# S5 steps of a four-branch trunk moved from GpSimd to VectorE, TensorE and ScalarE; convolution and rotary stage read PSUM

## The chip, the core and the metric

One core of one Trainium2 chip runs the whole program. The metric is the device time of an execution in microseconds; three executions of the kernel before give a median of 1277.6 us (1272.61 to 1278.52). "TensorE", "VectorE", "ScalarE", "GpSimd" and "SyncE" are PE, DVE, ACT, POOL and SP in the profile.

## The reference

A trunk of two layers over 272 tokens (16 learned ones and 256 of the input) of width 1024. Each layer normalizes, projects once into all inputs of four branches, runs the branches, weighs each by a sigmoid gate, adds them, projects, and ends with a squared-ReLU MLP of width 4096. The branches:

- *HGRN2*: attention with a decay per key channel; forget gate `f = lb + (1 - lb) * sigmoid(f_raw)`, key `1 - f`.
- *SSD* (Mamba-2): a causal convolution of four taps over 1024 channels, silu, then attention with a scalar decay.
- *S5*: a diagonal complex state space, 32 groups of 16 channels with 64 states: `x_t = a x_(t-1) + B u_t`, `y_t = Re(C x_t) + d * u_t`, then gelu and a gated linear unit.
- *Retention*: queries and keys are rotated (`x1 cos - x2 sin`, `x1 sin + x2 cos` on halves of 32 channels), then attention with a fixed decay.

All is float32.

## The kernel before

**Projections.** Weights come in 336 chunks of 128 x 1024 (`chunk`, line 307). ScalarE rounds a chunk to its high half (`whi`, L325), VectorE subtracts that from the chunk (`wlo`, L327), and TensorE multiplies (`gemm`, lines 333 to 351): per 128 rows of input, high x high (L344), high x low (L345) and low x high (L347), 24 matmul records a chunk, into one of three PSUM banks `g`. Other matmuls use the PSUM banks `ma`, `mb` (two each) and `mc` (one), and are in plain float32, which the profile shows as two records each.

**Order.** The program is written once in order; a planner then orders each engine's queue by priority and by its own estimates of when operands are there. The split of weights has a raised priority (`PS`, line 321). Each engine runs its queue in order. Loads of weights go through SyncE's queue; small loads (S5's parameters `raw`, the rotary tables) through ScalarE's.

**S5.** Time is cut into 68 steps of four tokens; the 512 channels are four blocks b of 128. `s5_params` (line 833, layer 0 only) computes powers of the state factor by well over a hundred small VectorE operations. Per block, `s5_prep` (line 995) loads the block's B and C, and forms outer products of parameters and B or C: `bs` and `cx[0]` on VectorE, `cx[1]` on GpSimd (`outer`, L1011 to L1013, 512 wide). `s5_table` (line 978) makes the rotation table E by six products of 288 on GpSimd (L987 to L992). TensorE and ScalarE form the short convolution `ki` (L1042 to L1048) and transpose `bs` (`bi`, L1059). `s5_run` (line 1099) multiplies the input W by `bi` into PSUM, turns it by E (L1115 to L1120), scans the two parts (L1128), turns back (L1132 to L1137; L1132 and L1135 on GpSimd), and sums `ki`, `cx` and the states into PSUM `yp` (L1143, L1146); VectorE adds `du`, the input times d, made on GpSimd (L1139, L1148). After two blocks `s5_out` (line 1150) applies gelu (L1154) and moves rows of 32 partitions into channel order by 16 copies, half on VectorE (L1160), half on ScalarE (L1162). At the end of `s5` all four parts are split into halves (L362, L364). Tiles of a block have one buffer each, so blocks follow one another. S5 runs beside the projections of the gates; its result is used much later, in `glu`. Block 0 of layer 1 is prepared in layer 0 (line 462).

**HGRN2 in.** `hgrn_in` (line 1185): after tanh on ScalarE, VectorE scales and shifts the forget gate (L1201) and GpSimd makes `1 - f` (L1202).

**Convolution.** In `ssd_in` (line 1329), for each of eight chunks ScalarE copies the projection out of PSUM (L1401) and makes the last tap (L1402); VectorE adds three taps from the copy (L1405).

**Rotary.** `ret_in` (line 1479): ScalarE copies four projections out of PSUM (L1489); then the two tables are loaded (L274), and GpSimd multiplies by the sine table with halves exchanged (four products of 32 partitions, L1496), by the cosine table (L1497), and adds (L1500, L1501).

Of the kernel before, what the change touches and what calls it, by code (L numbers as in the profile page):

```python
# [233 lines left out]
class Net:  # L234
# [760 lines left out]
    def s5_prep(self, l, b, after=None):  # L995
# [39 lines left out]
        nc.scalar.activation(nb, bs[:, 1, :, 3], AF.Copy, scale=-1.0)  # L1035

        def kd(pe=nullcontext(), act=nullcontext()):

            kp = self.bank("mc")[0:32].rearrange("p (q d x) -> p q d x", q=4, d=4)
            with pe:  # L1040
                for q in range(4):
                    nc.tensor.matmul(kp[:, q], lhsT=bs[:, 0, q, 3], rhs=cx[0][:, q, 0:4], start=True, stop=False)  # L1042
                    nc.tensor.matmul(kp[:, q], lhsT=nb[:, q], rhs=cx[1][:, q, 0:4], start=False, stop=True)
            for s in range(1, 4):
                g.memset(ki[32 * s:32 * s + 32, :, 0:s], 0.0)
            with act:
# [33 lines left out]
    def s5(self, l, W):  # L1080
        yf = self.slot(6, [128, 4, 68, 4])
        for b in range(4):
# [7 lines left out]
            self.s5_run(l, b, W, prep, Y[:, 4 * (b % 2):4 * (b % 2) + 4])  # L1090
            if b % 2:
                self.s5_out(b - 1, Y, yf)
        yf = yf.rearrange("p a c s -> p a (c s)")
        gh, gl = self.slot(9, [128, 4, T], F32R), self.slot(7, [128, 4, T], F32R)
        for i in range(4):
            self.split(yf[:, i], gh[:, i], gl[:, i])
        return gh, gl

    def s5_run(self, l, b, W, prep, Y):
# [38 lines left out]
        du = a1  # L1138
# [11 lines left out]
    def s5_out(self, b, Y, yf):  # L1150

# [3 lines left out]
        G = Y.rearrange("p (a q c) -> p a q c", a=2, q=4)  # L1155
        for q in range(4):
# [28 lines left out]
    def hgrn_in(self, l, raw, r, norm, t0):  # L1185
# [6 lines left out]
        for i in range(4):  # L1192
# [6 lines left out]
            nc.scalar.activation(f, f, AF.Tanh, scale=0.5)  # L1199
            a, b = (0.5, 0.5) if l == 0 else (self.omlb[:, i:i + 1], self.lb[:, i:i + 1])  # L1200
# [277 lines left out]

    def ret_in(self, l, u, t0):
        nc = self.nc  # L1480
        g = nc.gpsimd
        qk = self.slot(1, [128, 4, T])
        if t0:
            g.memset(qk[:, 0:2, 0:t0], 0.0)
# [5 lines left out]
        rot = [self.slot(k, [128, 4, T]) for k in (8, 2)]  # L1490
        for i in range(2):
            self.load_after(rot[i], self.io["rot"].rearrange("p (c k t) -> p c k t", c=2, k=4)[:, i], qk[:, 0:1, 0:1])
        sw = self.slot(13, [128, 4, T])
        for q in range(4):
            a, b = slice(32 * q, 32 * q + 32), slice(32 * (q ^ 1), 32 * (q ^ 1) + 32)
# [2 lines left out]
        qf, k = self.slot(14, [128, 4, T]), self.kpad[1]
        q = qf[:, 0:2]
        g.tensor_tensor(out=q, in0=qk[:, 0:2], in1=sw[:, 0:2], op=ALU.add)  # L1500
        g.tensor_tensor(out=k[:, :, 0:T], in0=qk[:, 2:4], in1=sw[:, 2:4], op=ALU.add)  # L1501
# [50 lines left out]
```

## Time and profile before

| | us |
|---|---|
| median of three executions | 1277.6 |
| lowest, highest | 1272.61, 1278.52 |
| the profiled execution, as timed | 1277.68 |
| its span, first to last instruction | 1275.9 |
| TensorE busy | 1216.1 |
| VectorE busy | 893.0 |
| ScalarE busy | 694.2 |
| GpSimd busy | 411.0 |

The profile is of one execution. Busy time of an engine is the time in which at least one of its instructions runs; matmuls overlap, and their ends are modelled. "Granted clock" is the share of full speed that the chip allowed TensorE. A stretch is given in microseconds from the start of the span. The S5 blocks of layer 0 run between about 150 and 300 us, those of layer 1 between about 800 and 925 us.

### The profile page before, as it was taken

How to read it: one execution, taken by the hardware profiler on the slowest of the kernel's cores; microseconds unless marked ns; L12 is line 12 of the kernel's file. 1: busy time of each engine (PE TensorE's matmuls, PEld its weight loads, DVE VectorE, ACT ScalarE, POOL GpSimd, SP SyncE). 2: the span in 40 equal slices, each digit the busy share in tenths (PEclk: the TensorE clock that was granted, in tenths of full speed). 3: DMA queues.
4: the chain of work that ended last, by engine and by line, in shares of the span. 5: the costliest groups of instructions: out<-in, count | busy, mean ns of one | idle time of the engine just before them, and what ended most of it. 6: DMA issues, size and time to landing. Idle time of an engine off the chain costs nothing.

```text
span 1275.9 us, 24312 instructions
## 1 busy us (share of the span) xinstructions
PE 1216.1 (95%) x9534; PEld 1174.6 (92%) x9534; DVE 893.0 (70%) x1480; ACT 694.2 (54%) x1219; POOL 411.0 (32%) x422
## 2 busy tenths in 40 slices
PE   8999998879999989999989999988999998999997
PEld 7999897879999989999979998987999998999996
DVE  8999989885637675544468995898656487655444
ACT  7446746443745665544455558354647546665442
POOL 2452467668002142200024333575170031322001
PEclk9999999989999989999989999998999998999998
DMA  6423232344354535555434332333444553555552
GB/s 238 160 98 104 101 123 99 108 136 145 135 175 173 176 110 178 173 175 178 170 108 143 126 123 97 123 111 114 146 150 149 184 179 136 169 188 189 182 184 98
DMA packets 53187, 186.69 MB, mean 146 GB/s; under 512 B 6096, under 2 KB 7248, under 8 KB 53072
## 3 DMA queue, kind: packets, MB, share of 16 engines
q1 hardware_dynamic: 50480, 179.40, 41.2%
q10 hardware_dynamic: 2592, 5.74, 1.4%
q8 instruction: 75, 1.23, 0.4%
q14 instruction: 40, 0.33, 0.1%
HBM read 184.06 MB, written 1.05 MB: 145 GB/s over the span
## 4 chain that ended last, share of the span: by engine, by line
PE 76%; DVE 13%; issue 4%; POOL 3%; ACT 2%; DMA 1%; SPq 0%; DVEq 0%; ACTq 0%; POOLq 0%
PE g L347 22%; PE g L344 22%; PE g L345 22%; DVE wlo L327 3%; PE mb L726 1%; PE ma L1263 1%; PE mb L717 1%; POOL S L1496 1%; DVE h L604 1%; DMA s5a<-in_bc 1%; DVE big_npom L601 1%; DVE s5a L1012 1%; ACT whi L325 1%; PE ma L726 1%; PE mb L1109 1%
## 5 line engine op out<-in xcount | busy, mean ns | idle before, releaser
L327 DVE TENSOR_TENSOR wlo<-wst,whi 128x1024 fp32r<-128x1024 f32 x336 | 438.5, 1306 | 259.1 <-PE g L347 220.8
L325 ACT ACTIVATE whi<-wst 128x1024 fp32r<-128x1024 f32 x336 | 355.8, 1060 | 365.3 <-PE g L345 287.6
L347 PE MATMUL g<-xh_u,wlo 128*128 128x272 f32 (+1 forms) x1024 | 299.7, 294 | 16.0 <-DVE wlo L327 15.8
L344 PE MATMUL g<-xh_u,whi 128*128 128x272 f32 (+1 forms) x1024 | 299.5, 293 | 0.6 <-ACT early L1068 0.4
L345 PE MATMUL g<-xl_u,whi 128*128 128x272 f32 (+1 forms) x1024 | 297.8, 291 | 0.0
L344 PE MATMUL g<-S,whi 128*128 128x272 f32 (+1 forms) x832 | 236.0, 288 | 4.6 <-ACT S L541 4.1
L347 PE MATMUL g<-S,wlo 128*128 128x272 f32 (+1 forms) x808 | 230.0, 288 | 1.7 <-DVE wlo L327 1.7
L345 PE MATMUL g<-S,whi 128*128 128x272 f32 (+1 forms) x768 | 220.4, 289 | 2.2 <-DVE S L552 1.9
L347 PEld LDWEIGHTS g<-xh_u,wlo 128*128 128x128 f32 x1024 | 195.7, 192 | 21.0 <-DVE wlo L327 18.2
L344 PEld LDWEIGHTS g<-xh_u,whi 128*128 128x128 f32 x1024 | 196.5, 192 | 2.6 <-ACT early L1068 0.7
L345 PEld LDWEIGHTS g<-xl_u,whi 128*128 128x128 f32 x1024 | 196.5, 192 | 1.5 <-issue 1.2
L344 PEld LDWEIGHTS g<-S,whi 128*128 128x128 f32 x832 | 157.1, 190 | 5.3 <-ACT S L541 4.5
L347 PEld LDWEIGHTS g<-S,wlo 128*128 128x128 f32 x808 | 151.9, 189 | 2.6 <-DVE wlo L327 2.2
L345 PEld LDWEIGHTS g<-S,whi 128*128 128x128 f32 x768 | 145.8, 190 | 4.1 <-DVE S L552 4.0
L345 PE MATMUL g<-xl_npm,whi 128*128 128x272 f32 (+1 forms) x512 | 147.7, 291 | 1.2 <-DVE xl_npm L552 1.2
L344 PE MATMUL g<-xh_npm,whi 128*128 128x272 f32 (+1 forms) x512 | 143.6, 289 | 2.4 <-ACT xh_npm L541 2.4
L347 PE MATMUL g<-xh_npm,wlo 128*128 128x272 f32 (+1 forms) x496 | 140.5, 288 | 0.0
L345 PEld LDWEIGHTS g<-xl_npm,whi 128*128 128x128 f32 x512 | 99.1, 193 | 1.9 <-DVE xl_npm L552 1.7
L344 PEld LDWEIGHTS g<-xh_npm,whi 128*128 128x128 f32 x512 | 96.7, 193 | 2.9 <-ACT xh_npm L541 2.9
L677 POOL TENSOR_TENSOR acc<-acc,tmp 128x272 f32<-128x272 f32 (+1 forms) x48 | 38.9, 828 | 186.0 <-DVE tmp L676 186.0
L347 PEld LDWEIGHTS g<-xh_npm,wlo 128*128 128x128 f32 x496 | 94.2, 192 | 0.2
L507 POOL TENSOR_TENSOR tmp<-tmp 128x272 f32<-128x272 f32 (+1 forms) x64 | 45.7, 714 | 137.3 <-DVE wlo L327 79.5
(377 smaller groups left out, 2184.4 us busy)
## 6 DMA issues: line engine op xcount, KB each, us to landing
wst<-in_w SPq DMA_DIRECT2D x336, 512.0 KB, 3.5
S<-in_rot ACTq DMA_DIRECT2D x4, 544.0 KB, 6.8
s5a<-in_bc ACTq DMA_DIRECT2D x8, 256.0 KB, 3.4
h<-in_h SPq DMA_DIRECT2D x4, 272.0 KB, 5.5
S<-in_ssdc ACTq DMA_DIRECT2D x2, 384.0 KB, 4.4
dtc<-in_ssdc ACTq DMA_DIRECT2D x2, 272.0 KB, 4.7
out<-h SPq DMA_DIRECT2D x2, 256.0 KB, 2.8
S<-in_lvl SPq DMA_DIRECT2D x1, 448.0 KB, 7.2
```

Source lines behind the costliest of these rows:

```text
L325: a = nc.scalar.activation(hi, st, AF.Copy)
L327: nc.vector.tensor_tensor(out=lo, in0=st, in1=hi.bitcast(F32), op=ALU.subtract)
L344: self.nc.tensor.matmul(out, lhsT=a, rhs=r, start=st, stop=False)
L345: self.nc.tensor.matmul(out, lhsT=a, rhs=s, start=False, stop=False)
L347: end = self.nc.tensor.matmul(out, lhsT=b, rhs=r, start=False, stop=en)
L507: nc.gpsimd.tensor_tensor(out=q, in0=a, in1=a, op=ALU.mult)
L601: e.tensor_tensor(out=mw[:, k], in0=mw[:, k], in1=r, op=ALU.mult)
L604: e.tensor_tensor(out=self.h[:, k, sl], in0=self.h[:, k, sl], in1=mw[:, k], op=ALU.add)
L677: nc.gpsimd.tensor_tensor(out=a, in0=a, in1=t, op=ALU.add)
L717: nc.tensor.matmul(ps[:, c0:c0 + T - q0], lhsT=k[b, 128 * s:128 * s + 128], rhs=q[b, q0:T], start=True, stop=True)
L726: nc.tensor.matmul(out[:, t:T], lhsT=v01[s] if s < 2 else v2, rhs=P[:, p0:p0 + T - t], start=s == 0, stop=s == 2)
L1012: e.tensor_tensor(out=tmp, in0=X[1 - r], in1=F[1], op=ALU.mult)
```

## The change

1. *Tables, preparation.* `s5_table` and the outer product for `cx[1]` go to VectorE. ScalarE makes the diagonal of d (four copies of 32 columns a block); TensorE adds it to `ki` by one more matmul per group, so that `du` is no longer needed.
2. *States.* In `s5_run`, one sum and two products go to VectorE, the broadcast `m4` to ScalarE; `du` is dropped, and ScalarE copies `yp` to Y.
3. *Output.* The 16 copies of `s5_out` become 32 matmuls by slices of the identity (128 rows, 32 outputs, 68 columns); the result is read from PSUM, for the first two blocks by a ScalarE copy, for the last two by the split itself.
4. *Parameters.* Some products of `s5_params` are done several at once: 18 operations fewer.
5. *Forget gates.* Both affine forms are made on ScalarE.
6. *Convolution.* VectorE's taps read the projection in PSUM; the copy is dropped.
7. *Rotary.* The tables are loaded before the projections, once `z` exists. VectorE multiplies each projection, in PSUM, by both tables; TensorE exchanges the halves by a permutation matrix (`swap`, 64 KB more of constants); VectorE adds from PSUM.

The core of the diff:

```diff
@@ s5_params
-        cmul(*P(3), *P(2), *P(1))
-        cmul(*P(4), *P(2), *P(2))
+        cmul(pw[:, 0, 3:5], pw[:, 1, 3:5], pw[:, 0, 1:3], pw[:, 1, 1:3],
+             *[x.unsqueeze(1).to_broadcast(sh) for x in P(2)])
...
-        for s in (2, 1, 0):
-            cmul(c5[:, 0, s], c5[:, 1, s], cR, cI, *P(3 - s))
+        cmul(c5[:, 0, 0:3], c5[:, 1, 0:3], *[pw[:, r, 3:0:-1] for r in range(2)],
+             *[x.unsqueeze(1).to_broadcast(sh) for x in (cR, cI)])
@@ s5_table
-        g = self.nc.gpsimd
+        g = self.nc.vector
@@ s5_prep
-        outer(g, self.pw[:, :, 1:5], R4[:, 2:4], cx[1][:, :, 1:5], view(tab2), 1)
+        outer(v, self.pw[:, :, 1:5], R4[:, 2:4], cx[1][:, :, 1:5], view(tab2), 1)
...
+        dd = slot[0][:, 912:1040].rearrange("p (q x) -> p q x", q=4)
+        for q in range(4):
+            nc.scalar.activation(dd[:, q], self.c("ident")[:, 0:32], AF.Copy, scale=self.p(l, "s5d", 4 * b + q))
...
-                    nc.tensor.matmul(kp[:, q], lhsT=nb[:, q], rhs=cx[1][:, q, 0:4], start=False, stop=True)
+                    nc.tensor.matmul(kp[:, q], lhsT=nb[:, q], rhs=cx[1][:, q, 0:4], start=False, stop=False)
+                    nc.tensor.matmul(kp[:, q, 0], lhsT=self.c("ident")[:, 0:32], rhs=dd[:, q], start=False, stop=True)
@@ s5
+            if b == 1:
+                for i, ps in enumerate(self.s5_out(Y)):
+                    nc.scalar.activation(yf[:, i], ps, AF.Copy)
...
+        for i, ps in enumerate(self.s5_out(Y)):
+            self.split(ps, cs(gh[:, 2 + i]), cs(gl[:, 2 + i]))
@@ s5_run
-        g.tensor_tensor(out=a1, in0=a1, in1=a2, op=ALU.add)
+        v.tensor_tensor(out=a1, in0=a1, in1=a2, op=ALU.add)
...
-        g.tensor_scalar(out=m4, in0=self.m4[:, l, pr].unsqueeze(2).to_broadcast([128, 4, 68]), scalar1=1.0, scalar2=None,
-                        op0=ALU.mult)
+        nc.scalar.activation(m4, self.m4[:, l, pr].unsqueeze(2).to_broadcast([128, 4, 68]), AF.Copy)
...
-        g.tensor_tensor(out=a1, in0=z[0], in1=eR, op=ALU.mult)
+        v.tensor_tensor(out=a1, in0=z[0], in1=eR, op=ALU.mult)
...
-        g.tensor_tensor(out=a3, in0=z[0], in1=eI, op=ALU.mult)
+        v.tensor_tensor(out=a3, in0=z[0], in1=eI, op=ALU.mult)
...
-        g.tensor_tensor(out=du, in0=W[:, pr], in1=self.p(l, "s5d")[:, pr].unsqueeze(2).to_broadcast([128, 4, 68]),
-                        op=ALU.mult)
...
-        v.tensor_tensor(out=Y, in0=yp, in1=du, op=ALU.add)
+        nc.scalar.activation(Y, yp, AF.Copy)
@@ s5_out
-                o, i = yf[32 * q:32 * q + 32, b:b + 2, :, s], G[32 * s:32 * s + 32, :, q, :]
-                if q % 2:
-                    nc.vector.tensor_copy(o, i)
-                else:
-                    nc.scalar.activation(o, i, AF.Copy)
+        for a in range(2):
+            ps = self.bank("mb")[:, :T].rearrange("p (s c) -> p s c", s=4)
             for s in range(4):
+                for q in range(4):
+                    nc.tensor.matmul(ps[32 * q:32 * q + 32, s], lhsT=self.c("ident")[:, 32 * s:32 * s + 32],
+                                     rhs=G[:, a, q], start=True, stop=True)
@@ hgrn_in
-            v.tensor_scalar(out=f, in0=f, scalar1=a, scalar2=b, op0=ALU.mult, op1=ALU.add)
-            g.tensor_scalar(out=KG[i // 2][:, i % 2], in0=f, scalar1=-1.0, scalar2=1.0, op0=ALU.mult, op1=ALU.add)
+            nc.scalar.activation(KG[i // 2][:, i % 2], f, AF.Identity, scale=c, bias=a if l else self.c05)
+            nc.scalar.activation(f, f, AF.Identity, scale=a, bias=b)
@@ ssd_in
-            nc.scalar.activation(x, ps, AF.Copy)
...
-                v.scalar_tensor_tensor(out=ac[:, d:T], in0=x[:, 0:T - d], scalar=cw[:, 4 * i + k:4 * i + k + 1],
+                v.scalar_tensor_tensor(out=ac[:, d:T], in0=ps[:, 0:T - d], scalar=cw[:, 4 * i + k:4 * i + k + 1],
@@ ret_in
-            nc.scalar.activation(qk[:, i, a:T], ps, AF.Copy)
...
-            g.tensor_tensor(out=sw[b], in0=qk[a], in1=rot[1][a], op=ALU.mult)
-        g.tensor_tensor(out=qk, in0=qk, in1=rot[0], op=ALU.mult)
...
+            for x, r in ((qs, rot[1]), (qc, rot[0])):
+                nc.vector.tensor_tensor(out=x[:, i, a:T], in0=ps, in1=r[:, i, a:T], op=ALU.mult)
+
+            ps = self.bank()[:, :T]
+            nc.tensor.matmul(ps, lhsT=self.c("swap"), rhs=qs[:, i], start=True, stop=True)
+            nc.vector.tensor_tensor(out=q[:, i] if i < 2 else k[:, i - 2, 0:T], in0=ps, in1=qc[:, i], op=ALU.add)
```

## Rows read from the trace of the kernel before

**Rows 1.** The page, head and part 1: busy time, share of span, instructions.

```profile
span 1275.9 us, 24312 instructions
...
PE 1216.1 (95%) x9534; PEld 1174.6 (92%) x9534; DVE 893.0 (70%) x1480; ACT 694.2 (54%) x1219; POOL 411.0 (32%) x422
```

**Rows 2.** Busy time by stretch: us, busy of each engine (instructions), granted clock, DMA.

```profile
150.00:300.00 150.00, 132.72 (x995) 124.88 (x994) 126.00 (x171) 74.75 (x145) 104.22 (x99) 0.97 0.35 117
800.00:925.00 125.00, 113.04 (x881) 108.11 (x880) 102.92 (x151) 63.48 (x116) 65.80 (x70) 0.95 0.37 123
...
500.00:625.00 125.00, 125.00 (x993) 125.00 (x992) 60.91 (x65) 61.79 (x91) 11.71 (x18) 1.00 0.51 176
25.00:150.00 125.00, 123.79 (x985) 117.63 (x985) 124.69 (x382) 75.49 (x142) 49.87 (x41) 1.00 0.36 123
```

**Rows 3.** Waits in 150 to 300 us: total us, times, longest.

```profile
PE g L347 <- DVE wlo L327: 10.7, 5, 2.9
...
DVE S L1118 <- POOL s5e L992: 1.1, 1, 1.1
```

**Rows 4.** VectorE groups by form in 150 to 300 us: xcount, busy us, mean ns.

```profile
L327 DVE TENSOR_TENSOR wlo<-wst,whi 128x1024 fp32r<-128x1024 f32 x30 | 48.6, 1621 | 14.6 <-PE g L347 8.7 <-issue 5.9
...
L1011 DVE TENSOR_TENSOR s5g<-s5a,s5c 128x512 f32<-128x512 f32 x8 | 6.2, 816 | 0.0
...
L1160 DVE COPY S<-S 32x136 f32<-32x136 f32 x16 | 4.8, 303 | 0.2
L1012 DVE TENSOR_TENSOR s5a<-s5a,s5p 128x512 f32<-128x512 f32 x4 | 4.7, 1163 | 0.0
L1137 DVE SCALAR_TENSOR_TENSOR s5d<-S 128x272 f32<-128x272 f32 x4 | 3.8, 941 | 0.0
...
L1120 DVE TENSOR_TENSOR S<-S 128x272 f32<-128x272 f32 x4 | 2.1, 536 | 0.0
```

**Rows 5.** The same in 800 to 925 us.

```profile
L327 DVE TENSOR_TENSOR wlo<-wst,whi 128x1024 fp32r<-128x1024 f32 x26 | 37.0, 1422 | 12.4 <-PE g L347 11.0 <-ACT whi L325 1.1 <-issue 0.3
...
L1011 DVE TENSOR_TENSOR s5g<-s5a,s5c 128x512 f32<-128x512 f32 x6 | 3.9, 679 | 0.0
```

**Rows 6.** The same in 500 to 625 us.

```profile
L327 DVE TENSOR_TENSOR wlo<-wst,whi 128x1024 fp32r<-128x1024 f32 x42 | 51.5, 1225 | 43.3 <-PE g L347 41.3 <-issue 1.4
```

**Rows 7.** VectorE groups by form over the whole span.

```profile
L845 DVE TENSOR_TENSOR s5b<-s5b 128x32 f32<-128x32 f32 x68 | 13.1, 216 | 0.0
...
L1405 DVE SCALAR_TENSOR_TENSOR S<-S,half 128x271 f32<-128x271 f32 x16 | 10.5, 658 | 0.0
...
L676 DVE SCALAR_TENSOR_TENSOR tmp<-S,g 128x272 f32<-128x272 f32 x24 | 9.9, 427 | 2.0 <-PE g L347 2.0
```

**Rows 8.** TensorE in order of time: start us, us from first start to last end.

```profile
117.77 0.87 PE L726 MATMUL ma<-S,S 128*128 128x272 f32 x4
...
119.54 0.37 PE L347 MATMUL g<-xh_u,wlo 128*128 128x272 f32 x1
...
138.40 0.29 PE L345 MATMUL g<-xl_u,whi 128*128 128x272 f32 x1
138.62 0.67 PE L726 MATMUL mb<-S,S 128*64 128x272 f32 x4
...
139.54 0.39 PE L347 MATMUL g<-xh_u,wlo 128*128 128x272 f32 x1
```

**Rows 9.** The chain of waits, in order of time: start us, us, records.

```profile
808.90 1.75 PE mb L1109 x16
```

**Rows 10.** ScalarE groups by form over the whole span.

```profile
L1162 ACT ACTIVATE S<-S 32x136 f32<-32x136 f32 x32 | 14.2, 445 | 0.4
```

**Rows 11.** The page, part 6: DMA issues, KB each, us to landing.

```profile
S<-in_rot ACTq DMA_DIRECT2D x4, 544.0 KB, 6.8
```

**Rows 12.** GpSimd groups over the whole span: largest of S5's, smallest of the tables'.

```profile
L1013 POOL TENSOR_TENSOR s5c<-s5c,s5d 128x512 f32<-128x512 f32 x8 | 14.5, 1810 | 0.2
...
L992 POOL TENSOR_TENSOR s5e<-s5e 128x288 f32<-128x288 f32 x8 | 8.1, 1013 | 0.5
```

More of the change, by code (lines that the diff above doesn't have):

```diff
@@ L71 @@
 _n = 0
-for _name, _w in (("ident", 128), ("ones", 128), ("cen", 128), ("m432", 432), ("he", 1), ("ho", 1), ("le", 1), ("lo", 1),
+for _name, _w in (("ident", 128), ("ones", 128), ("cen", 128), ("swap", 128), ("m432", 432), ("he", 1), ("ho", 1), ("le", 1), ("lo", 1),
                   ("rh", 1), ("rl", 1), ("r1", 1)):
@@ L105, in shape_constants @@
     put("cen", np.eye(128) - 1.0 / 128)
+    put("swap", np.eye(128)[p ^ 32])
     t = np.arange(T)
@@ L388, in run @@
         nc.vector.memset(self.eps, EPS)
+        self.c05 = self.cp.tile([128, 1], F32, name="c05")
+        nc.vector.memset(self.c05, 0.5)
         nc.scalar.preload_act_table_set("natural_log")
@@ L463, in layer @@
         G = self.gates(l, B_SSD, u_sl, N, (10, 12))
-        rt = self.ret_in(l, u_all, t0)
+        rt = self.ret_in(l, u_all, t0, z[:, 0:1, 0:1])
         self.merge(l, B_SSD, ysd, G, sl, False)
@@ L803, in scalars @@
         v.tensor_scalar(out=self.lb, in0=self.lb, scalar1=0.5, scalar2=0.5, op0=ALU.mult, op1=ALU.add)
+        self.nomlb = e[:, 0:4]
+        v.tensor_scalar(out=self.nomlb, in0=self.omlb, scalar1=-1.0, scalar2=None, op0=ALU.mult)
         self.stp = self.cp.tile([128, DEPTH, 17], F32, name="stp")
@@ L922, in s5_params @@
         cmul(*P(2), *P(1), *P(1))
-        cmul(*P(3), *P(2), *P(1))
-        cmul(*P(4), *P(2), *P(2))
+        sh = [128, 2, DEPTH, 16]
+        d = d4[:, 0:64].rearrange("p (i l q) -> p i l q", i=2, l=DEPTH)
+        cmul(pw[:, 0, 3:5], pw[:, 1, 3:5], pw[:, 0, 1:3], pw[:, 1, 1:3],
+             *[x.unsqueeze(1).to_broadcast(sh) for x in P(2)])
         c5 = self.cp.tile([128, 2, 4, DEPTH, 16], F32, name="s5c")
@@ L942, in s5_params @@
         tt(cI, cI, inv, ALU.mult)
-        for s in (2, 1, 0):
-            cmul(c5[:, 0, s], c5[:, 1, s], cR, cI, *P(3 - s))
+        sh = [128, 3, DEPTH, 16]
+        d = d4[:, 0:96].rearrange("p (i l q) -> p i l q", i=3, l=DEPTH)
+        cmul(c5[:, 0, 0:3], c5[:, 1, 0:3], *[pw[:, r, 3:0:-1] for r in range(2)],
+             *[x.unsqueeze(1).to_broadcast(sh) for x in (cR, cI)])
+        d = new()
         self.eb = self.cp.tile([128, 2, DEPTH, 16, 8], F32, name="s5eb")
@@ L1080, in s5 @@
     def s5(self, l, W):
-        yf = self.slot(6, [128, 4, 68, 4])
+        nc = self.nc
+        yf = self.slot(6, [128, 2, 68, 4])
         for b in range(4):
@@ L1090, in s5 @@
             self.s5_run(l, b, W, prep, Y[:, 4 * (b % 2):4 * (b % 2) + 4])
-            if b % 2:
-                self.s5_out(b - 1, Y, yf)
-        yf = yf.rearrange("p a c s -> p a (c s)")
+            if b == 1:
+                for i, ps in enumerate(self.s5_out(Y)):
+                    nc.scalar.activation(yf[:, i], ps, AF.Copy)
         gh, gl = self.slot(9, [128, 4, T], F32R), self.slot(7, [128, 4, T], F32R)
-        for i in range(4):
-            self.split(yf[:, i], gh[:, i], gl[:, i])
+        cs = lambda a: a.rearrange("p (c s) -> p c s", s=4)
+        for i in range(2):
+            self.split(yf[:, i], cs(gh[:, i]), cs(gl[:, i]))
+        for i, ps in enumerate(self.s5_out(Y)):
+            self.split(ps, cs(gh[:, 2 + i]), cs(gl[:, 2 + i]))
         return gh, gl
@@ L1131, in s5_run @@
         sR, sI = st[:, 0, :, 1:69], st[:, 1, :, 1:69]
-        g.tensor_tensor(out=a1, in0=z[0], in1=eR, op=ALU.mult)
+        v.tensor_tensor(out=a1, in0=z[0], in1=eR, op=ALU.mult)
         v.tensor_tensor(out=a2, in0=z[1], in1=eI, op=ALU.mult)
         v.tensor_tensor(out=sR, in0=a1, in1=a2, op=ALU.subtract)
-        g.tensor_tensor(out=a3, in0=z[0], in1=eI, op=ALU.mult)
+        v.tensor_tensor(out=a3, in0=z[0], in1=eI, op=ALU.mult)
         v.tensor_tensor(out=a4, in0=z[1], in1=eR, op=ALU.mult)
         v.scalar_tensor_tensor(out=sI, in0=a3, scalar=-1.0, in1=a4, op0=ALU.mult, op1=ALU.subtract)
-        du = a1
-        g.tensor_tensor(out=du, in0=W[:, pr], in1=self.p(l, "s5d")[:, pr].unsqueeze(2).to_broadcast([128, 4, 68]),
-                        op=ALU.mult)
         yp = self.bank("mb")[:, :T].rearrange("p (q c) -> p q c", q=4)
@@ L1147, in s5_run, with s5_out @@
                                  rhs=st[:, r, q, 0:68], start=False, stop=(r == 1))
-        v.tensor_tensor(out=Y, in0=yp, in1=du, op=ALU.add)
-    def s5_out(self, b, Y, yf):
+        nc.scalar.activation(Y, yp, AF.Copy)
+    def s5_out(self, Y):
         nc = self.nc
@@ L1155, in s5_out @@
         G = Y.rearrange("p (a q c) -> p a q c", a=2, q=4)
-        for q in range(4):
+        out = []
+        for a in range(2):
+            ps = self.bank("mb")[:, :T].rearrange("p (s c) -> p s c", s=4)
             for s in range(4):
-                o, i = yf[32 * q:32 * q + 32, b:b + 2, :, s], G[32 * s:32 * s + 32, :, q, :]
-                if q % 2:
-                    nc.vector.tensor_copy(o, i)
-                else:
-                    nc.scalar.activation(o, i, AF.Copy)
+                for q in range(4):
+                    nc.tensor.matmul(ps[32 * q:32 * q + 32, s], lhsT=self.c("ident")[:, 32 * s:32 * s + 32],
+                                     rhs=G[:, a, q], start=True, stop=True)
+            out.append(ps.rearrange("p s c -> p c s"))
+        return out
     def glu(self, l, x, ks, sl):
@@ L1199, in hgrn_in @@
             nc.scalar.activation(f, f, AF.Tanh, scale=0.5)
-            a, b = (0.5, 0.5) if l == 0 else (self.omlb[:, i:i + 1], self.lb[:, i:i + 1])
-            v.tensor_scalar(out=f, in0=f, scalar1=a, scalar2=b, op0=ALU.mult, op1=ALU.add)
-            g.tensor_scalar(out=KG[i // 2][:, i % 2], in0=f, scalar1=-1.0, scalar2=1.0, op0=ALU.mult, op1=ALU.add)
+            a, b, c = (0.5, self.c05, -0.5) if l == 0 else (self.omlb[:, i:i + 1], self.lb[:, i:i + 1],
+                                                           self.nomlb[:, i:i + 1])
+            nc.scalar.activation(KG[i // 2][:, i % 2], f, AF.Identity, scale=c, bias=a if l else self.c05)
+            nc.scalar.activation(f, f, AF.Identity, scale=a, bias=b)
         if t0:
@@ L1399, in ssd_in @@
             slot = self.slot(13 + i % 2, [128, 4, T])
-            x, ac, th = (slot[:, i] for i in range(3))
-            nc.scalar.activation(x, ps, AF.Copy)
+            ac, th = (slot[:, i] for i in range(2))
             nc.scalar.activation(ac, ps, AF.Identity, scale=cw[:, 4 * i + 3:4 * i + 4], bias=cb[:, i:i + 1])
@@ L1476, in ssd_fin, with ret_in @@
         return yh, yl
-    def ret_in(self, l, u, t0):
+    def ret_in(self, l, u, t0, dep):
         nc = self.nc
         g = nc.gpsimd
-        qk = self.slot(1, [128, 4, T])
+        qc, qs = self.slot(1, [128, 4, T]), self.slot(13, [128, 4, T])
+        rot = [self.slot(k, [128, 4, T]) for k in (8, 2)]
+        for i in range(2):
+            self.load_after(rot[i], self.io["rot"].rearrange("p (c k t) -> p c k t", c=2, k=4)[:, i], dep)
+        qf, k = self.slot(14, [128, 4, T]), self.kpad[1]
+        q = qf[:, 0:2]
         if t0:
-            g.memset(qk[:, 0:2, 0:t0], 0.0)
+            g.memset(qc[:, 0:2, 0:t0], 0.0)
+            g.memset(qs[:, 0:2, 0:t0], 0.0)
         for i in range(4):
@@ L1488, in ret_in @@
             ps = self.proj(l, (O_RQ, O_RQ + 128, O_RK, O_RK + 128)[i], (u[0], u[1], slice(a, T)), T - a)
-            nc.scalar.activation(qk[:, i, a:T], ps, AF.Copy)
[L1490 to L1495, printed above, removed]
-            g.tensor_tensor(out=sw[b], in0=qk[a], in1=rot[1][a], op=ALU.mult)
-        g.tensor_tensor(out=qk, in0=qk, in1=rot[0], op=ALU.mult)
[L1498 to L1501, printed above, removed]
+            for x, r in ((qs, rot[1]), (qc, rot[0])):
[3 more added lines that the diff above has]
+            nc.vector.tensor_tensor(out=q[:, i] if i < 2 else k[:, i - 2, 0:T], in0=ps, in1=qc[:, i], op=ALU.add)
         v01, v2 = self.slot(0, [128, 2, 4, 128]), self.vpad[0].rearrange("p (i e) -> p i e", i=4)
```

## The prediction

> **What bounds the kernel now.** I read the page first: TensorE is busy 95% of the span, VectorE 70%, ScalarE 54%, GpSimd 32% [rows 1]. So the time is TensorE's own work plus what TensorE loses. The profiled execution took 1277.7 us outside, 1275.9 us of it span; the median of the runs is 1277.6 us, so the sum below, made against 1277.7, needs no shift.
>
> Next I looked for where TensorE loses, in the table of stretches [rows 2]. In the up/down stage (500 to 625 us) it has work all 125 us at full clock. In 25 to 150 us it lacks 1.2 us of 125. In the two S5 stages it doesn't: in 150 to 300 us (layer 0) it is busy 132.7 of 150 us, and the granted clock is 0.97; in 800 to 925 us (layer 1) 113.0 of 125 us, at 0.95. Idle: 17.3 + 12.0 = 29.3 us. The granted clock has two levels here, 2.4 and 1.2 GHz, so a mean of 0.97 means work lost for 3% of the stretch: 4.5 us, and 6.3 us in layer 1. **Loss in both S5 stages: about 40 us.**
>
> Then what ends these waits. In the first stage the largest is the low half of the split weights, `wlo`, which VectorE makes: 10.7 us in 5 waits, while VectorE itself waits for GpSimd hardly at all (1.1 us) [rows 3]. So VectorE is late not because it waits but because it is full and its operations are long. By form: the `wlo` subtraction takes 1621 ns in the first S5 stage, 1422 ns in the second and 1225 ns in the up/down stage, where GpSimd is almost idle [rows 2, 4 to 6]. S5's 512-wide operations with two SBUF operands take from 816 to 1163 ns in layer 0 (38 of them, six groups; the slowest and the fastest are shown) against 679 ns for the fastest group of layer 1 [rows 4, 5]. S5's 272-wide ones with two SBUF operands take from 536 to 941 ns (five groups of 4) [rows 4]; those that read PSUM keep 427 ns [rows 7]. GpSimd is busy 104.2 of the 150 us in just that stretch [rows 2]. I read this as the two engines slowing one another when VectorE takes both operands from SBUF.
>
> **The change part by part.**
>
> *VectorE, relief.* If the GpSimd work of S5 goes, layer 0 gets back on `wlo` 30 x (1.621 - 1.225) = 11.9 us; on the 38 wide ones 38 x (0.99 - 0.68) = 11.8 us (0.99 is the middle of the six groups); on 20 of the 272-wide 20 x (0.74 - 0.43) = 6.2 us: 29.9 us. Layer 1 goes by its `wlo`: 26 x (1.422 - 1.225) = 5.1 us, 0.43 of layer 0, so 12.9 us. Of 42.8 us I take 36, as GpSimd keeps the SSD products, the memsets and the sums of the merges. Nothing shows how much is left, so the ends are 18 and 42.8.
>
> *VectorE, load.* Each of 8 preparations adds six 288-wide products (6 x 0.45, from the 272-wide 427 ns) and three 512-wide (3 x 0.68): 4.74 us, 37.9 in all. Each of 8 runs adds three 272-wide and drops the sum with `du`: 2 x 0.43, 6.9 us. The partition-shifting copies go: 4.8 us per layer, 9.6 [rows 4]. Net 35.2 us. Rotary adds 24 of 0.43: 10.3 us, beyond the busiest part. So the load about equals the relief, and VectorE stays as full as it is. What changes is that its queue consists of operations that last what they last alone. The planner that orders the queues puts `wlo` ahead of S5's work; an operation that is stretched in the middle delays every `wlo` behind it, and TensorE with it. In 25 to 150 us VectorE is busy 124.7 of 125 us and TensorE loses 1.2 [rows 2]: a full VectorE need not starve TensorE.
>
> *TensorE, loss given back.* Between nothing and 37.3 us (the 40 us less what 25 to 150 us loses, scaled to 275 us: 2.7). I take two thirds of the 40: **26.7 us back.** Two thirds because the waits for the S5 parameters' transfer and the serial steps inside a block stay.
>
> *TensorE, new work.* It is in-order and full, so what it gets beyond the recovered idle time is paid. Prices per column from two groups of 12 records (1728 columns): full width 117.77 to 119.54 us, 1.77 us, 1.02 ns; outputs of 64 partitions 138.62 to 139.54 us, 0.92 us, 0.53 ns, two tiles side by side [rows 8]. S5's output shuffle: 128 matmuls of 32 x 68, two records each, 17,408 columns x 0.53 = 9.3 us; low end a quarter of full width, 4.5; high end 256 records at the 1.75 / 16 us of S5's state matmuls, 28.0 us [rows 9]. I take the 64-wide price, the nearest in shape. The diagonal term: 32 matmuls of 32 columns, 2048 x 1.02 = 2.1 us (1.1 to 7.0, by the same two rows). The rotary swap: 8 of 272, 4352 x 1.02 = 4.5 us. **Together +15.9 us (10.1 to 39.5).**
>
> By the Trainium skill, "TensorEngine Tiling (Array Packing)", section Tiling Modes, changing the tiling mode drains the engine; that is a rule against this shuffle and belongs to the rival on its price. The trace bears it out mildly: from the last full-width matmul at 138.40 to the first 64-wide at 138.62 us are 0.22 us, where two full-width ones inside a chunk are 0.126 us apart [rows 2, 8].
>
> *Edits that cost about nothing.* The convolution reads PSUM: 16 x (658 - 427) ns = 3.7 us less on VectorE for the widest of three groups [rows 7]; the bank is held until the third operation, about 1.3 us later, in a rotation of three banks that TensorE fills in some 3.0 us each (24 records of 125/993 us [rows 2]). If VectorE lags by more than that, TensorE waits for the bank: up to 16 x 1.3 = 21 us. S5's parameters lose 18 operations of 216 ns, 3.9 us [rows 7]. The forget gates' affine leaves VectorE and GpSimd. All three lie mostly where TensorE loses only 1.2 us: I take -1 us (0 to -2 without the bank). Were VectorE's cover gone there, the 21 us is the price.
>
> By the Trainium skill, "VectorE: DVE Perf Modes", section Rules for kernel authors, PSUM should be copied to SBUF first if many operations follow. Here the rows say otherwise (427 ns from PSUM, 658 from SBUF beside GpSimd); by the rule the 1 us gained would be a loss of a few.
>
> ScalarE drops 32 copies of 445 ns [rows 10], 16 of the convolution and 8 of rotary, and gets some 68 small ones (diagonals, `m4`, Y, the affine): about even at 54% busy. The rotary tables are asked for before the projections; they land in 6.8 us [rows 11] and eight gate chunks of 3 us lie between. VectorE's first product now waits for them, and every `wlo` is queued behind it: if late, TensorE stalls at once, but the cover is 24 us. The longer constant load adds 64 KB to 421, at the start: some tenths. What GpSimd gives up, from the largest S5 group to the smallest of the tables' [rows 12], was on no wait that TensorE shows.
>
> **Sum:** 1277.7 - 26.7 + 15.9 - 1.0 = 1265.9, **1266 us.**
>
> **The rivals.**
> 1. *VectorE becomes the pacer (slower).* The stretching has other causes too (strides, ScalarE), and only 18 us of relief come. Then VectorE's load rises by 35.2 + 10.3 - 18 = 27.5 us. Its idle time in the two stages is 24.0 + 22.1 us, half of it forced by transfers and TensorE, so half the rise lengthens the stages: 1277.7 + 13.8 = 1291 us. For: `wlo` is the wait today and rotary isn't offset. Against: PSUM readers are not stretched. It decides below some 25 us of relief. Chance 0.12.
> 2. *TensorE pays full price for the small matmuls (slower).* Each 32-wide shuffle pays drains and weight loads: 39.5 instead of 15.9 us, 1277.7 - 26.7 + 39.5 - 1 = 1289.5, 1290 us. For: 109 ns per record in the state matmuls. Against: the 64-wide group. Chance 0.08; by the Trainium skill's drain rule (same section) it would be likelier.
> 3. *Off the path (no change).* Only a third of the loss comes back, as the S5 chain stays serial: 1277.7 - 13.3 + 15.9 - 1 = 1279 us. Chance 0.20.
> 4. *All of it.* 37.3 us back and the low price: 1277.7 - 37.3 + 10.1 - 1 = 1249.5, 1250 us. Chance 0.15.
> The forecast keeps 0.45.
>
> **How the numbers follow.** A measurement here tells about 0.5%, 6.4 us: faster is below 1271.2, slower above 1284. Faster: forecast and rival 4, 0.60; same: rival 3, 0.20; slower: rivals 1 and 2, 0.20. The range runs from rival 4 to rival 2, 1250 to 1289 us: half of rival 4 lies below, somewhat more than half of 1 and half of 2 above, under 0.2 together; it holds the ends of VectorE's relief and most of TensorE's.
>
> **What would show it.** Right: `wlo` near 1.25 us in the S5 stages, S5's wide operations near 0.7, TensorE idle there under 12 us, few dips of the clock; GpSimd below 250 us; a shuffle of 64 records in 2 to 3 us. Wrong: `wlo` still over 1.4 us (rival 1); shuffle groups of 6 us or more (rival 2); TensorE's waits for `wlo` unchanged with unstretched operations (rival 3); waits for a projection bank in the convolution, or VectorE waiting for the rotary tables (the two edits I put at nothing).

## The result and the profile after

The changed kernel takes 1257.0 us (median of four runs, 1256.8 to 1259.1) against 1277.1 us for the kernel before on the same chip (1272.6 to 1278.5): 0.985 of before, 95% interval 0.983 to 0.988. It is faster; the forecast was 1266.0 us, 9 us too much.

The page's head, after [rows 1]:

```profile
span 1255.4 us, 24880 instructions
...
PE 1212.4 (97%) x9870; PEld 1176.3 (94%) x9870; DVE 864.5 (69%) x1536; ACT 692.5 (55%) x1232; POOL 215.6 (17%) x289
```

GpSimd works half as long. TensorE has 336 records more, yet is busy 3.7 us less, at a mean granted clock of 0.989 against 0.980: fewer of them run at the lower level. The stretches, after [rows 2]: TensorE's idle time in the S5 stretches falls from 17.3 and 12.0 us to 2.8 and 0.7, at a clock of 1.00. But in 25 to 150 us, where TensorE lacked 1.2 us before, it now lacks 9.1, at 0.96.

```profile
150.00:300.00 150.00, 147.18 (x1285) 141.13 (x1283) 124.52 (x219) 83.79 (x166) 16.10 (x29) 1.00 0.42 136
800.00:925.00 125.00, 124.31 (x1144) 119.83 (x1143) 98.20 (x177) 68.00 (x133) 11.06 (x26) 1.00 0.44 143
...
25.00:150.00 125.00, 115.86 (x897) 109.44 (x896) 117.34 (x363) 67.95 (x134) 37.68 (x38) 0.96 0.32 105
```

Fixed stretches hold different work in the two kernels. For a balance the span is cut where the same weight chunk's `wlo` starts: S5's first projection chunk and retention's output chunk, in each layer. First before, then after (same columns):

```profile
25.00:91.80 66.80, 65.98 (x541) 63.59 (x541) 66.79 (x209) 33.38 (x57) 33.08 (x28) 1.00 0.38 135
91.80:295.10 203.30, 185.62 (x1404) 174.69 (x1403) 181.60 (x343) 114.18 (x224) 116.26 (x109) 0.97 0.34 114
295.10:739.90 444.80, 433.93 (x3375) 425.37 (x3374) 276.19 (x379) 236.07 (x393) 97.84 (x112) 0.98 0.45 154
739.90:931.00 191.10, 178.97 (x1376) 167.83 (x1376) 149.17 (x228) 110.51 (x213) 92.94 (x86) 0.96 0.36 119
931.00:1275.00 344.00, 331.01 (x2714) 324.47 (x2712) 197.88 (x245) 182.34 (x302) 65.53 (x75) 0.98 0.49 166
```

```profile
25.00:104.40 79.40, 72.93 (x570) 70.29 (x569) 79.37 (x263) 35.88 (x62) 23.13 (x27) 0.94 0.35 115
104.40:291.40 187.00, 181.52 (x1548) 172.68 (x1547) 158.97 (x318) 111.73 (x229) 29.87 (x39) 1.00 0.38 125
291.40:736.10 444.70, 432.53 (x3389) 424.17 (x3388) 271.45 (x388) 237.83 (x397) 80.63 (x105) 0.99 0.48 154
736.10:911.50 175.40, 174.65 (x1532) 166.15 (x1531) 138.06 (x246) 106.58 (x212) 23.88 (x35) 1.00 0.41 132
911.50:1255.00 343.50, 329.52 (x2714) 323.04 (x2712) 195.84 (x245) 182.23 (x302) 53.28 (x70) 0.99 0.51 165
```

The lengths change by +12.6, -16.3, -0.1, -15.7 and -0.5 us, together -20.0. **Three quarters of the gain of layer 0's S5 stage are eaten by the stage ahead of it (12.6 of 16.3 us); layer 1 keeps its own.** Counting idle time and (1 - clock) x length as loss, the S5 stages lose 23.8 and 19.8 us before, 5.5 and 0.8 after: 37.3 back. The first stage loses 0.8 before, 11.2 after. The clock is shown to 0.01, so each of these losses is good to about 1 us.

VectorE in 150 to 300 us, by form, after [rows 4], then `wlo` in 800 to 925 us [rows 5]:

```profile
L328 DVE TENSOR_TENSOR wlo<-wst,whi 128x1024 fp32r<-128x1024 f32 x36 | 44.9, 1246 | 19.4 <-PE g L348 9.7 <-ACT whi L326 6.0 <-issue 3.7
...
L1021 DVE TENSOR_TENSOR s5g<-s5a,s5c 128x512 f32<-128x512 f32 x8 | 5.2, 688 | 2.2 <-PE mc L1056 1.2 <-PE mb L699 0.9
...
L1023 DVE TENSOR_TENSOR s5b<-s5b,s5a 128x512 f32<-128x512 f32 x4 | 2.7, 683 | 0.0
...
L997 DVE TENSOR_TENSOR s5e<-s5ea,s5eb 128x288 f32<-128x288 f32 x4 | 1.8, 448 | 0.0
...
L1155 DVE SCALAR_TENSOR_TENSOR s5d<-S 128x272 f32<-128x272 f32 x4 | 1.7, 432 | 0.0
```

```profile
L328 DVE TENSOR_TENSOR wlo<-wst,whi 128x1024 fp32r<-128x1024 f32 x31 | 37.8, 1220 | 16.6 <-PE g L348 11.7 <-issue 3.6 <-ACT S L661 1.0
```

`wlo` went from 1621 and 1422 ns to 1246 and 1220. The product of line 1155 (L1137 before) went from 941 to 432 ns, and VectorE does 36 splits in this stretch instead of 30. TensorE's waits in 150 to 300 us [rows 3] no longer name `wlo`:

```profile
PE mb L729 <- ACT S L1458: 1.5, 1, 1.5
PE mb L1176 <- ACT S L1169: 1.1, 1, 1.1
```

TensorE in order of time shows the new shuffle (one of four, which waits for nothing) and a swap (one of eight), each between matmuls of a projection; then the whole span's groups of both:

```profile
271.37 0.29 PE L346 MATMUL g<-xl_u,whi 128*128 128x272 f32 x1
271.58 1.16 PE L1176 MATMUL mb<-S,cst 128*32 128x68 f32 x64
272.67 0.39 PE L348 MATMUL g<-xh_u,wlo 128*128 128x272 f32 x1
272.90 0.29 PE L345 MATMUL g<-xh_u,whi 128*128 128x272 f32 x1
...
273.90 0.29 PE L348 MATMUL g<-xh_u,wlo 128*128 128x272 f32 x1
274.02 0.62 PE L1517 MATMUL ma<-S,cst 128*128 128x272 f32 x2
274.28 0.49 PE L345 MATMUL g<-xh_u,whi 128*128 128x272 f32 x1
274.61 0.29 PE L346 MATMUL g<-xl_u,whi 128*128 128x272 f32 x1
```

```profile
L1517 PE MATMUL ma<-S,cst 128*128 128x272 f32 x16 | 5.1, 398 | 0.0
L1176 PE MATMUL mb<-S,cst 128*32 128x68 f32 x256 | 4.6, 224 | 1.2 <-ACT S L1169 1.1
```

The new loss shows in TensorE's waits in 25 to 150 us, and in its order of time:

```profile
PE ma L1282 <- DVE S L1345: 6.1, 2, 3.8
PE ma L1300 <- DVE S L1345: 1.6, 1, 1.6
```

```profile
79.49 2.05 PE L1282 MATMUL ma<-S,S 128*128 128x128 f32 x8 [3.84 <-DVE S L1345]
...
82.08 0.43 PE L346 MATMUL g<-xl_u,whi 128*128 128x272 f32 x1
...
85.32 0.29 PE L346 MATMUL g<-xl_u,whi 128*128 128x272 f32 x1
```

HGRN2's score matmuls wait 3.8 us for an operand that VectorE scales (L1345), and afterwards the projection's matmuls take 0.43 us instead of 0.29, at the lower clock, until 85.3 us: one wait is paid twice. VectorE is busy throughout: 50.0 us of 75 to 125 us (below).

### The profile page after: what moved, and what is told of

The parts are those of the page before. It is cut to its first block, busy times and chain, and to the rows that moved or that the text cites. A ratio compares the mean times of both kernels' runs of the same rounds, so it can differ in the third digit from the quotient of the medians.

```text
span 1255.4 us, 24880 instructions
## 1 busy us (share of the span) xinstructions
PE 1212.4 (97%) x9870; PEld 1176.3 (94%) x9870; DVE 864.5 (69%) x1536; ACT 692.5 (55%) x1232; POOL 215.6 (17%) x289
## 4 chain that ended last, share of the span: by engine, by line
PE 81%; DVE 11%; ACT 4%; issue 2%; POOL 1%; DMA 0%; SPq 0%; ACTq 0%; DVEq 0%
PE g L345 24%; PE g L346 24%; PE g L348 24%; DVE wlo L328 2%; PE mb L729 1%; PE mb L1128 1%; PE mb L1161 1%; DVE S L1423 1%; ACT whi L326 1%; DVE S L1291 1%; DVE h L607 1%; ACT S L1092 1%; DVE xl_npm L555 1%; DVE big_npom L604 1%; DVE big_npost L604 1%
## 5 line engine op out<-in xcount | busy, mean ns | idle before, releaser
L328 DVE TENSOR_TENSOR wlo<-wst,whi 128x1024 fp32r<-128x1024 f32 x336 | 418.5, 1247 | 272.1 <-PE g L348 223.6
L348 PE MATMUL g<-xh_u,wlo 128*128 128x272 f32 (+1 forms) x1024 | 296.5, 291 | 0.0
```

The lines of the kernel that those rows point to most:

```text
L328: nc.vector.tensor_tensor(out=lo, in0=st, in1=hi.bitcast(F32), op=ALU.subtract)
L348: end = self.nc.tensor.matmul(out, lhsT=b, rhs=r, start=False, stop=en)
```

## Experiments

Line numbers shift by a few between kernels. "Before" is each job's own set of runs (1278.7, 1276.9 and 1278.1 us).

**1. GpSimd gets its S5 work back.** In the changed kernel:

```diff
-        g = self.nc.vector                                  # s5_table
+        g = self.nc.gpsimd
-        outer(v, ..., cx[1][:, :, 1:5], view(tab2), 1)
+        outer(g, ..., cx[1][:, :, 1:5], view(tab2), 1)
-        v.tensor_tensor(out=a1, in0=a1, in1=a2, op=ALU.add) # and the products a1, a3; m4 likewise
+        g.tensor_tensor(out=a1, in0=a1, in1=a2, op=ALU.add)
```

> The changed kernel with tables, one outer product, the states' sums and products and m4 back on GpSimd (du stays gone; shuffle, convolution, rotary, affine as changed). Theory C (contention): wlo in the S5 stages back at 1.4 to 1.6 us, S5's wide operations 0.8 to 1.1 us, TensorE idle there again over 15 us: ratio about 0.998 to 1.004, most of the gain gone. Rival D (the gain comes from the shuffle, du and rotary): ratio 0.985 to 0.990.

1290.3 us, 1.009 of before (1.007 to 1.012). That is slower than theory C's 0.998 to 1.004: without the move of S5's GpSimd work the other edits are a loss, and the move is worth some 31 us (1.009 less 0.985, of 1278). In 150 to 300 us:

```profile
150.00:300.00 150.00, 138.52 (x1165) 133.18 (x1165) 120.38 (x160) 77.03 (x150) 74.04 (x80) 0.95 0.38 119
```

TensorE lacks 11.5 us again, while VectorE is busy *less* (120.4 against 124.5) with 59 operations fewer. So the load moved onto VectorE isn't what counts. But this run mixes two costs: `wlo` lasts 1346 ns in this stretch (1355 in 800 to 925 us), a little under the 1.4 us expected, and TensorE waits 6.4 us for `wlo`, but also 5.0 us for steps of S5 itself (3.1 of them for the state products of L1153). The next run separates them.

**2. Ballast on GpSimd.** No computation of S5 goes back; GpSimd multiplies constants into a scratch tile, 17 products of 272 per block that no other instruction reads. A copy of one column ahead of each series ties it to its block.

```diff
+        for n in (272,) * 12:     # after s5_table; 5 more in s5_run
+            g.tensor_tensor(out=self.scr[:, 0:n], in0=self.c("m432")[:, 0:n], in1=self.c("m432")[:, 0:n], op=ALU.mult)
```

> The changed kernel with useless GpSimd products added beside each S5 preparation (12 of 272) and run (5 of 272), from constants into a scratch tile that nobody reads; one copy of a column ties them to the block. About 136 of some 0.8 us, 110 us of GpSimd. Theory C: VectorE's two-operand work from SBUF is stretched, wlo over 1.4 us in the S5 stages, 8 to 20 us slower than the changed kernel, ratio 0.991 to 1.0. Rival D (waiting on GpSimd's results was the cost): nothing waits for them, ratio 0.984 to 0.987.

1300.6 us, 1.018 of before (1.015 to 1.021): some 42 us above the changed kernel, far more than expected. Stretches; then, in 150 to 300 us, VectorE by form and TensorE's largest wait:

```profile
150.00:300.00 150.00, 137.92 (x1155) 131.31 (x1154) 142.63 (x209) 76.77 (x151) 75.79 (x104) 0.95 0.37 118
800.00:925.00 125.00, 108.46 (x918) 103.67 (x919) 112.77 (x173) 61.41 (x124) 73.59 (x89) 0.93 0.38 121
```

```profile
L328 DVE TENSOR_TENSOR wlo<-wst,whi 128x1024 fp32r<-128x1024 f32 x31 | 42.8, 1380 | 7.1 <-ACT whi L326 4.5 <-PE g L348 1.3 <-issue 1.3
...
L1024 DVE TENSOR_TENSOR s5b<-s5b,s5a 128x512 f32<-128x512 f32 x4 | 4.6, 1157 | 0.0
```

```profile
PE g L348 <- DVE wlo L328: 11.6, 7, 4.2
```

VectorE has fewer operations in 150 to 300 us (209 against 219) and is busy 18 us longer; the 512-wide product takes 1157 ns instead of 683, and TensorE waits for `wlo` again (11.6 us, and 12.2 us in 800 to 925 us). **That busy GpSimd stretches VectorE's operations is shown, by itself.** Not all of the 42 us need be that: in layer 1 TensorE also waits 4.3 us for a step of SSD's output norm (L1492) that stands between ballast products on GpSimd, and ScalarE waits 3.3 and 2.4 us for ballast instructions: the one-column copies read a tile of S5 that it writes next (L1041).

**3. The shuffle back to copies.** The matmuls of `s5_out` give way to the 16 copies per call of the kernel before.

> The changed kernel with the 16 copies per two blocks in place of the shuffle on TensorE. Its trace shows the 64 records of a shuffle in 1.16 us, so about 4 us of TensorE in all. Theory S (shuffle cheap, copies on a full VectorE dear): 2 to 8 us slower than the changed kernel, ratio 0.987 to 0.992. Rival P (TensorE is the bound, so its 4 us count and the copies hide): 2 to 5 us faster, 0.981 to 0.984.

1261.9 us, 0.988 (0.986 to 0.990): by the ratio 3 us slower than with matmuls, as theory S had it, but the intervals overlap, so it isn't shown that the matmuls are better. In 800 to 925 us VectorE is busy 1.7 us more and ScalarE 5.3 us more, and TensorE is idle for 5.2 us, at 0.97. 3.5 us of that are one wait for GpSimd's step of SSD's output norm; that the copies made it late isn't shown:

```profile
800.00:925.00 125.00, 119.85 (x983) 115.45 (x982) 99.94 (x188) 73.26 (x146) 9.91 (x24) 0.97 0.44 137
```

```profile
PE ma L1479 <- POOL S L1477: 3.5, 1, 3.5
```

**4. The convolution alone**, in the kernel before:

```diff
-            nc.scalar.activation(x, ps, AF.Copy)
-                v.scalar_tensor_tensor(out=ac[:, d:T], in0=x[:, 0:T - d], ...
+                v.scalar_tensor_tensor(out=ac[:, d:T], in0=ps[:, 0:T - d], ...
```

> The kernel before with only the convolution changed (taps read PSUM, no copy). Theory H: TensorE waits in the convolution, 8 to 13 us slower, ratio 1.006 to 1.010. Rival V: within 3 us of the kernel before, 0.998 to 1.002, as VectorE saves 2 us and ScalarE 6 us that nothing waits for.

1283.7 us, 1.0044 of before (1.0032 to 1.0057): slower, between the two theories' ranges; the `wlo` of layer 0's retention output chunk starts 9.1 us later, and a part returns in layer 1. VectorE's taps became cheaper (484 to 486 ns against 534 to 658), yet TensorE now waits in 25 to 150 us, for HGRN2's operand and not for a projection bank:

```profile
PE ma L1263 <- DVE S L1326: 4.1, 3, 2.0
```

**5. The convolution undone**, in the changed kernel (the same lines back).

> The changed kernel with the convolution's ScalarE copy back, the taps reading SBUF. In the changed kernel TensorE loses 8.2 us idle and 5 us of clock in 75 to 125 us, where the kernel before lost 1.0. Theory H (bank hold): the taps hold the projection banks behind a full VectorE; with the copy back that loss goes, ratio to the kernel before about 0.975 (some 1245 us), weights of the first O_S5 chunk split at about 92 us as before instead of 104. Rival V (VectorE has more of S5's work there, or the queue order is another): 0.983 to 0.990, chunk still at 100 us or later.

1256.0 us, 0.983 (0.980 to 0.985); TensorE at 43.4 us of 75 to 125 us, at 0.93. That is rival V's time, though the first S5 chunk is split at 94.9 us and not at 100 or later. Most of the new loss in this stretch stays: the convolution isn't its only cause.

**6 and 7. Forget gates and convolution undone; then S5's parameters too.** The second kernel differs from the first by 18 small VectorE operations *more*.

> The changed kernel with convolution and forget gates as before, parameters as changed. Theory E with the forget gates as its part: loss in 25 to 150 us of 1 to 5 us, ratio 0.975 to 0.980. Rival Q: 8 to 14 us, ratio 0.982 to 0.987. If this is good and the kernel with all three put back is not, or the other way round, the order of the queues decides, not one edit.

> The changed kernel with convolution, forget gates and parameters as before. With the convolution alone put back, 25 to 150 us still lose 11 us of TensorE (7.4 idle, 3.75 by the clock; 14 in the changed kernel, 1.2 in the kernel before). Theory E (the early edits made that loss): it falls to 1 to 4 us, ratio 0.974 to 0.979. Rival Q (S5's work on VectorE, which now begins there, and the queue order planned around it): it stays at 8 to 14 us, ratio 0.982 to 0.987.

1256.2 us, 0.983 (0.981 to 0.985), and **1250.8 us, 0.979 (0.977 to 0.981)**. Of 75 to 125 us, before, after, and the kernel with all three undone:

```profile
75.00:125.00 50.00, 49.04 (x396) 46.96 (x395) 49.74 (x120) 28.96 (x58) 18.43 (x12) 1.00 0.34 116
```

```profile
75.00:125.00 50.00, 41.80 (x304) 39.48 (x306) 50.00 (x163) 17.39 (x41) 10.73 (x13) 0.90 0.22 73
```

```profile
75.00:125.00 50.00, 47.13 (x379) 44.98 (x379) 49.86 (x119) 27.42 (x57) 13.80 (x11) 1.00 0.36 108
```

The first is rival Q's time, the second theory E's. With the three undone the clock stays up, and layer 0's S5 stage ends 7 us earlier than in the changed kernel. The three edits meant to save a little cost some 8 us together (0.985 less 0.979); their intervals don't overlap.

**8. Only the parameters undone**, to see whether batching alone did it, by its place in VectorE's queue.

> After, with S5's parameter products one power at a time again (18 more small VectorE operations); convolution, forget gates, rotary and S5 stages as changed. Theory Q, order of VectorE's queue: in the written program HGRN's masks of its score blocks (the ones TensorE's next score matmuls wait for) stand later in VectorE's queue once the parameters are batched: the fourth to the seventh has 63.7, 65.3, 67.8 and 71.8 us of estimated VectorE work ahead of it in the changed kernel, 60.9 to 66.3 us in the kernel before, and 61.1 to 66.5 us here, as if nothing had changed. By Q the loss of 25 to 150 us goes: TensorE busy there over 120 of 125 us at a clock of 0.98 or more, no wait of 2 us or more on line L1345, time 0.977 to 0.981 of before, about 1250 us. Rival R, VectorE's amount of work: 18 operations more can only make it worse, TensorE stays at 115 to 117 us, and the time is 0.984 to 0.988.

1256.1 us, 0.984 (0.982 to 0.985). Theory Q fell: by the expectation's count the masks are at the old places in VectorE's queue, yet the loss is still there (43.5 us, 0.90). R's time came, but R can't hold either: experiment 7 has more VectorE operations still (1562 against 1554) and the least loss.

**9. Parameters and forget gates undone**, so that only the convolution differs from experiment 7.

> After, with S5's parameters and the forget gates as before; convolution and rotary as changed. It differs from the kernel with three edits back only in the convolution that reads PSUM. In VectorE's queue the later masks stand a little earlier than there, and the convolution holds its bank. Theory C2, the held bank costs: 2 to 6 us slower than the three-edit kernel (0.981 to 0.984). Rival, only the order matters: the same as that kernel, 0.977 to 0.981.

1258.4 us, 0.985 (0.983 to 0.986): by the ratio 7 us slower than experiment 7, by the convolution alone, with as many VectorE operations (1562); theory C2 had 2 to 6. But TensorE doesn't wait for a bank here, it waits for HGRN2's operand again (6.0 us, L1338). What Q had overlooked stands in TensorE's queue. Counted in the traces, in layer 0: the projection matmuls (24 a chunk) ahead of the eighth to twelfth group of HGRN2's score matmuls (eight records of 128 columns each):

```
before                           434  434  477  477  502
experiment 7 (all three undone)  434  434  479  479  502
convolution alone, in before     408  432  432  456  456
9, and 8                         408  432  432  456  456
after                            408  432  432  432  449
6 (parameters still batched)     456  456  476  476  504
5 (convolution undone)           456  456  480  480  480
```

Where the taps read PSUM, the planner puts these groups up to two chunks (some 6 us) earlier, so TensorE comes to them sooner, while VectorE, nearly full, isn't ready. With the taps reading SBUF and the parameters batched (5 and 6) most of the groups come as late as before or up to a chunk later, but in 6 TensorE waits 4.8 us for VectorE's last step of the convolution (L1426). Every departure from the old order lost. That the order is the cause is read from this table: no run changed the order alone, and why the planner chose so wasn't tested.

**10 to 12. The rotary stage undone:** in the changed kernel; with the parameters; with all three early edits.

> The changed kernel with rotary as before: 40 us of GpSimd again, 8 matmuls of 272 columns (some 4 us of TensorE) and 24 VectorE products fewer. Theory C (contention): what GpSimd stretches costs more than the 4 us, 0 to 6 us slower, ratio 0.985 to 0.990. Rival P: the 4 us come back, ratio 0.981 to 0.984.

> After, with only S5's parameters and the rotary stage as before; convolution and forget gates as changed. By theory Q with rotary's gain added: 0.975, about 1246 us. If the convolution's held bank costs by itself (it cost 0.4% in the kernel before), this is 2 to 5 us slower than the kernel with all four edits back: 0.977 to 0.980.

> After, with convolution, forget gates, S5's parameters and rotary stage all as before: only the S5 stages as changed. If the two gains seen singly add (the three early edits back 0.979, rotary back 0.9814, the changed kernel 0.9852 of before): 0.975, about 1246 us, with TensorE at 121 us or more of 125 in 25 to 150 us. If rotary's gain was only part of the same loss (its stage sits right behind layer 0's S5): 0.979, the same as with the three edits alone, about 1250 us.

1253.4 us, 0.981 (0.979 to 0.984); 1252.7 us, 0.980 (0.979 to 0.982); 1252.0 us, 0.980 (0.978 to 0.981). The first is rival P's time. The first two are some 3.5 to 5 us faster than the same kernels with the rotary moved (the changed kernel, experiment 8), at the edge of their intervals; the third is the same as experiment 7. So moving the rotary stage earns nothing here, and what undoing it gives in the first two doesn't add to the gain of experiment 7. Whether it costs anything by itself stays open. The best versions are 7 and 12, S5's move with the early edits undone.

## Why the prediction was right, and where not

The direction, the mechanism in the S5 stages and the range held. The terms:

- *VectorE, relief and load.* Right. `wlo` was to be near 1.25 us, S5's wide operations near 0.7: 1.246 and 0.68. The 288-wide products cost 448 ns where 0.45 us was taken. "The load about equals the relief" held only in a stretch of equal length (VectorE is busy 124.5 of 150 us against 126.0), which now holds more of the program's work. Over the span VectorE is busy 28.5 us less [rows 1], where the prediction's terms nearly cancel: relief was larger, or load smaller, than priced. `wlo` alone fell by 20.0 us (438.5 to 418.5), against 17.0 in the sum.
- *Loss given back: 26.7 us, two thirds.* Mis-sized. 37.3 us came back, the high end and rival 4's value. The reason for the missing third, "the waits for the S5 parameters' transfer and the serial steps inside a block stay", failed: in the changed kernel TensorE's named waits in 150 to 300 us sum to less than 3 us, so the serial chain was covered by projections once `wlo` came on time. The waits themselves stayed, but on VectorE, which still waits 3.5 us there for the transfer of B and C, against 6.4 before. Rival 3 falls with it.
- *TensorE, new work: 15.9 us.* Mis-sized. The shuffle is busy 4.6 us in all instead of 9.3, the named low end of 4.5, as I had taken the 64-wide price; the swap 5.1 instead of 4.5. But busy times of such groups overlap with their neighbours'. Counted as what they put between two projection matmuls, which otherwise start 0.126 us apart, a shuffle costs 1.28 us (271.37 to 272.90, less two steps) and a swap 0.46 (273.90 to 274.61); a diagonal matmul takes 0.06. That makes 5.1, 3.7 and 1.9: 10.7 us, near the low end of 10.1. By the balance the whole came to about 7.5 us: 5.3 us that the two S5 stages are longer than their returned loss explains, and some 2.2 that moved into the first stage (29 records more there). With losses good to 1 us a stage the two counts don't exclude one another; either is well below 15.9. Rival 2 falls: 64 records in 1.16 us. By the Trainium skill, "TensorEngine Tiling (Array Packing)", section Tiling Modes, a change of mode drains the engine; this trace shows a small price: the step into the shuffle is 0.21 us (271.37 to 271.58), into the full-width swap 0.12 (273.90 to 274.02).
- *"Edits that cost about nothing": -1 us.* Wrong, and the step that failed in kind. I priced a held bank and a missing cover ("Were VectorE's cover gone there, the 21 us is the price"), but took the stretch as safe because it lost only 1.2 us. By the table of experiment 9 it was safe only in that order of the queues, with VectorE full. The first stage lost 10.4 us more; with the three edits undone it loses 1.7 (experiment 7), and the kernel is some 8 us faster. The wait came up at HGRN2's scores, not at a bank; nor does VectorE wait for the rotary tables, the other sign that the prediction named.
- By the Trainium skill, "VectorE: DVE Perf Modes", section Rules for kernel authors, an operation on a matmul's output either accepts the PSUM read's rate or, if many operations follow, PSUM is copied to SBUF first. For these three taps experiment 4 agrees with the copy, but not because the reads from PSUM are dear: a tap of 271 columns takes 484 ns from PSUM against 658 from the copy [rows 7].

```profile
L1423 DVE SCALAR_TENSOR_TENSOR S<-g,half,S 128x271 f32<-128x271 f32 x8 | 3.9, 484 | 0.0
```

- *Rival 1, VectorE the pacer.* Not in the S5 stages; in the stage ahead, by other edits.

Summed by the balance, whose terms are parts of one length and so must add up: 10.6 us more given back, 8.4 us less new work, 11.4 us more lost ahead: 8 of the 9 us by which the forecast was off. Two mis-sized terms ran one way and one the other; the total is closer than they are, and that is luck. The S5 move by itself behaved as rival 4, given a chance of 0.15: without the three early edits the kernel takes 1250.8 us (experiment 7), with rival 4's 1250 beside it.

## What to carry to other kernels

Where VectorE and GpSimd both work from SBUF, as here, the price of a GpSimd operation is also what it adds to VectorE's (683 to 1157 ns for a 512-wide product): it can pay to take it off, even at the cost of more VectorE work. Look at mean durations and not at busy shares. A stretch in which a full engine starves nobody may hold only by its order: an edit there that saves time on that engine can still lose, so measure each alone. Undo singly what came bundled with the large gain.

## What was not expected

GpSimd products that nobody reads, 136 in the program, cost some 42 us. And a wait of 3.8 us on TensorE cost more than itself: in 75 to 85 us of the changed kernel the granted clock was 0.66, a mix of the 1.2 and 2.4 GHz levels.

```profile
75.00:85.00 10.00, 5.95 (x28) 5.48 (x29) 10.00 (x25) 2.43 (x5) 1.42 (x2) 0.66 0.27 97
```
